# Scores in two steps for each pair of heads instead of three, with another division of the eight PSUM banks

## The chip, the cores and the metric

The kernel runs on one core of one Trainium2 chip. The metric is the device time of one execution in microseconds. The engines' names in the profile are PE (TensorE, its weight loads shown apart as PEld), DVE (VectorE), ACT (ScalarE), POOL (GpSimd) and SP (SyncE, which here only issues DMAs).

## The reference

A trunk of two layers over 512 positions of width 1024, and a last RMSNorm. In each layer one projection of the normalized input feeds three causal mixers, whose gated outputs are projected, merged by sigmoid gates, projected again and added to the input. All data is float32.

```python
def hybrid_layer(x, positions, ...):
    h = rmsnorm(x, norm_g)
    proj = jnp.einsum('bsd,dc->bsc', h, w_in)
    aq, ak, av, az, buv, bz, cq, ck, cv, cz, gl = split_cols(proj)
    ...
    oa = diff_attention(qa, ka, va, lam)      # A: 4 heads, two softmaxes each
    ya = (rmsnorm(oa, subln_g) * (1.0 - lam_init)).reshape(B, S, A_WIDTH) * jax.nn.silu(az)
    ...
    yb = u * mixed.reshape(B, S, B_WIDTH) * jax.nn.silu(bz)      # B: spatial gating
    ...
    yc = oc.reshape(B, S, C_WIDTH) * jax.nn.silu(cz)             # C: 8 heads, dilated windows
    pb = jnp.einsum('nbsc,ncd->nbsd', jnp.stack([ya, yb, yc]), w_branch)
    merged = jnp.einsum('bsnd,nbsd->bsd', jax.nn.sigmoid(gates), pb)
    return x + jnp.einsum('bsd,de->bse', merged, w_out)
```

In A, `p0 - lam * p1` of two causal softmaxes multiplies v. In C the three dilated patterns come out as one softmax with a count of 0 to 3 at each position.

## The kernel before

**Dense work.** Every float32 product is made of three matmuls of rounded parts (`mm3`, L412: high by high, high by low, low by high). The weights come from HBM in units of 512 KB (`raw`, two buffers, L151). `weights` (L176) splits each into six slots `whi`, `wlo` ahead of its use: ACT rounds (L170), DVE or POOL subtracts (L171). Most projections of two column blocks use Strassen's scheme with seven products (`seven`, L507); their weights come as one "S" group, for which `weights` takes two more buffers, `t12` and `t34`, from the tag "pr", and forms sums in them (L192 to L195). The tag "pr" has two buffers, and the softmax of the attention uses the same two. `seven` also uses one of the two buffers of the tag "sh" for as long as it runs.

**Order.** `plan` (L50) lists the items of a layer: the value projections (`i_vb`, `i_val`, all four position blocks at once in four PSUM banks), projections and attention A, attention C, then gates, branch outputs and the output projection. The attention functions call `fill`, which pulls a fixed share (`budget / FILLS`) of the dense items between their own steps, and `need`, which pulls until an item that they use is done. Tile's scheduler orders the instructions of each engine by priority before the run; scores (L870) and weight splits are lifted by 300 places.

**Attention.** `attention_a` and `attention_c` run over four pairs of heads, and over three steps for each pair, `STEPS = ((0, 1), (2,), (3,))`: the query blocks of 128 whose scores are made together. Block i has (i + 1) * 128 keys. In `scores` each block has six matmuls, three for each head of the pair (64 rows of the array each), into the two banks of one `ps_s`. DVE adds the mask and finds the row maximum (L882), ACT takes the exponential (L886); A then joins the two heads (L897) and C scales each (L904). One step later the result is transposed on PE (L910), copied by ACT (A, L935) or split by ACT and DVE (C, L418 and L419), and multiplied by v (L941, L1015). In C the two halves of the query positions are written to one bank for each head, and both banks are emptied after block 3 (L1023, L1024).

**PSUM.** Eight banks: `ps_pj` two, `ps_s` one tile of two, `ps_to` four. The sums of the first norm also pass through `ps_s` (`rms_spread`, L400): a bank of it holds the broadcast norm until ACT has copied it to `rbc` (L577).

Of the kernel before, what the change touches and what calls it, by code (L numbers as in the profile page):

```python
# [19 lines left out]
P = 128  # L20
# [16 lines left out]
FILLS = 25  # L37
STEPS = ((0, 1), (2,), (3,))
# [62 lines left out]
def hybrid_kernel(ctx: ExitStack, tc, xT, posr, wpack, tabs, cvec, pvec, rvec, lamv, sguw, outT):  # L101
# [16 lines left out]
    to_p = pool("to", bufs=4, space=PSUM)  # L118
# [10 lines left out]
    def ps_s():  # L129

        return s_p.tile([P, 2, S], F32, tag="s", name="ps_s")

    def ps_to():
        return to_p.tile([P, S], F32, tag="to", name="ps_to")

# [416 lines left out]
    def layer(l, xu, parts):  # L552
# [197 lines left out]
        def i_gl2(n, d):  # L750
# [5 lines left out]
            yield from pair(("gl2", n, d), use, ps_pj if (n, d) in ((BR_B, 0), (BR_A, 0)) else ps_to)  # L756
# [99 lines left out]
        def scores(br, h, step, r0=None):  # L856
# [3 lines left out]
            at, w0 = {}, 0  # L860
            for i in step:
                at[i] = slice(w0, w0 + (i + 1) * P)
                w0 = at[i].stop
            for i in step:
                qs = slice(i * P, (i + 1) * P)
                W = (i + 1) * P
                for t, (a, b) in enumerate(((0, 1), (1, 0), (0, 0))):
                    for m in range(2):
                        with tc.high_priority(offset=PRIO):
                            T.matmul(  # L870
                                pss[:, m, at[i]], lhsT=q[HALF[m], a, qs], rhs=k[HALF[m], b, :W], start=t == 0,
                                stop=t == 2,
                            )
            pr = t4k("pr", 2)
            rds = {}
            for i in step:
# [3 lines left out]
                for m in range(2):  # L880
                    o = pr[:, m, at[i]]
                    V.tensor_tensor_reduce(  # L882
                        out=o, in0=pss[:, m, at[i]], in1=tab[:, 0 if br == BR_A else 1, S - W :], op0=ALU.add,
# [7 lines left out]
                if br == BR_A:  # L891
# [6 lines left out]
                        out=pr[:, 0, at[i]], in0=pr[:, 1, at[i]], scalar=c, in1=pr[:, 0, at[i]], op0=ALU.mult,  # L898
                        op1=ALU.add,
                    )  # L900
                else:
                    for m in range(2):
                        o = pr[:, m, at[i]]
                        A.activation(out=o, in_=o, func=AF.Copy, scale=rd[:, m : m + 1])  # L904
            return {i: (pr[:, :, at[i]], rds[i]) for i in step}
# [7 lines left out]
        def attention_a(fill):  # L913
# [4 lines left out]
            for n in range(13):  # L918
                cur = None
                if n < 12:  # L920
                    h, step = n // 3, STEPS[n % 3]
                    need(*(("pp", BR_A, i_) for i_ in NEEDS[h]))
                    if n % 3 == 0:
                        po = ps_to().rearrange("p (i e) -> p i e", i=4)
# [4 lines left out]
                if prev is not None:  # L929
                    h, prs, po_, r0_, so_ = prev  # L930
                    pTs = {}
                    for i, (pr, rd) in prs.items():
                        pt = transposed(pr, 0, i)
                        pTs[i] = pT = att.tile([P, 4, P], F32, tag="pth", bufs=3, name="pT")
                        A.activation(out=pT[:, : i + 1, :], in_=pt, func=AF.Copy)  # L935
                    if late and 0 not in prs:
                        late.pop(0)()
                    fill()
                    for i, pT in pTs.items():
# [10 lines left out]
                    if 3 in prs:  # L950
# [21 lines left out]
                        late.extend((lambda: ons.append(scaled()), finish))  # L972
# [3 lines left out]
        def attention_c(fill):  # L976
# [3 lines left out]
            for n in range(13):  # L980
                cur = None
                if n < 12:
                    h, step = n // 3, STEPS[n % 3]
                    need(*(("pp", BR_C, i_) for i_ in NEEDS[h]))
                    if n % 3 == 0:
                        po = [ps_to() for _ in range(2)]
                    if n % 3 < 2:
                        pts = []
                        for m in range(2):
                            ph = att.tile([P, 4, 256], F32R, tag="pth", bufs=3, name="pth")  # L990
                            pl = att.tile([P, 4, 256], F32R, tag="ptl", bufs=3, name="ptl")
                            for t in (ph, pl):
                                G.memset(t[:, step[0] + 1, 0:P].bitcast(F32), 0.0)
                            pts.append((ph, pl))
                    cur = (h, scores(BR_C, h, step), po, pts)
# [3 lines left out]
                if prev is not None:  # L999
                    h, prs, po_, pts_ = prev  # L1000
                    for m in range(2):
                        for i, (pr, _) in prs.items():
                            pt = transposed(pr, m, i)
                            o = slice((i % 2) * P, (i % 2 + 1) * P)
                            split(pts_[m][0][:, : i + 1, o], pts_[m][1][:, : i + 1, o], pt)
                        fill(0.5)
                    i = max(prs)
                    if i % 2:
                        need(("val", BR_C))
                        v = val[BR_C]  # L1010
                        c = slice((i - 1) * P, (i + 1) * P)
                        for m in range(2):
                            for j in range(i + 1):
                                for s_, pt in enumerate(pts_[m]):
                                    T.matmul(  # L1015
                                        po_[m][:, c], lhsT=v[:, j, 2 * h + m, :], rhs=pt[:, j, :],
                                        start=j + s_ == 0, stop=j == i and s_ == 1,
                                    )
                    if i == 3:
                        need(("pp", BR_C, NEEDS_Z[h]))  # L1020
                        ob = t2k("ob")
                        for m in range(2):
                            A.activation(out=ob[HALF[m]], in_=po_[m][64:128], func=AF.Copy)  # L1023
                            V.tensor_tensor(out=ob[HALF[m]], in0=po_[m][0:64], in1=ob[HALF[m]], op=ALU.add)  # L1024
                        V.scalar_tensor_tensor(
                            out=yf[:, h, :], in0=ob, scalar=0.5, in1=qk[BR_C, h, "z"], op0=ALU.mult, op1=ALU.mult
                        )
# [131 lines left out]
```

## Time and profile before

| | before |
|---|---|
| median of 3 runs | 1108.19 us (1108.16 to 1108.91) |
| time of the profiled execution | 1109.62 us |
| its span, first to last instruction | 1107.9 us |
| PE busy / weight loads (PEld) busy | 1084.2 us (98%) / 938.0 us (85%) |
| DVE, ACT, POOL busy | 813.7 us (73%), 605.9 us (55%), 472.4 us (43%) |
| instructions | 17842 |

A busy engine is one with an instruction of its own running. The span of a matmul runs to its modelled end, so the spans of neighbours overlap, and how fast PE goes is read from the starts.

### The profile page before, as it was taken

How to read it: one execution, taken by the hardware profiler on the slowest of the kernel's cores; microseconds unless marked ns; L12 is line 12 of the kernel's file. 1: busy time of each engine (PE TensorE's matmuls, PEld its weight loads, DVE VectorE, ACT ScalarE, POOL GpSimd, SP SyncE). 2: the span in 40 equal slices, each digit the busy share in tenths (PEclk: the TensorE clock that was granted, in tenths of full speed). 3: DMA queues.
4: the chain of work that ended last, by engine and by line, in shares of the span. 5: the costliest groups of instructions: out<-in, count | busy, mean ns of one | idle time of the engine just before them, and what ended most of it. 6: DMA issues, size and time to landing. Idle time of an engine off the chain costs nothing.

```text
span 1107.9 us, 17842 instructions
## 1 busy us (share of the span) xinstructions
PE 1084.2 (98%) x6452; PEld 938.0 (85%) x6452; DVE 813.7 (73%) x1512; ACT 605.9 (55%) x1313; POOL 472.4 (43%) x418
## 2 busy tenths in 40 slices
PE   7999999999998999999999999999999999999997
PEld 6887878878887999998888888888788889999886
DVE  6678878877969877775427768788688797787544
ACT  6654757586774444444434456575867654444430
POOL 4004343433524766653310344534343446667420
PEclk9999999999999999999999999999999999999998
DMA  5431313220312333344523213122112133323433
GB/s 196 136 123 58 96 58 96 87 66 20 115 39 77 96 114 90 101 137 153 188 95 114 95 45 109 58 96 77 58 39 76 58 97 113 100 93 112 135 110 100
DMA packets 35064, 105.97 MB, mean 96 GB/s; under 512 B 4704, under 2 KB 7776, under 8 KB 34976
## 3 DMA queue, kind: packets, MB, share of 16 engines
q1 hardware_dynamic: 29936, 98.50, 27.9%
q10 hardware_dynamic: 5040, 6.34, 1.8%
q8 instruction: 51, 0.84, 0.3%
q14 instruction: 37, 0.30, 0.1%
HBM read 100.58 MB, written 4.24 MB: 95 GB/s over the span
## 4 chain that ended last, share of the span: by engine, by line
PE 88%; DVE 5%; issue 2%; DMA 2%; ACT 2%; POOL 1%; SPq 0%; POOLq 0%; DVEq 0%; ACTq 0%
PE ps_pj L413 15%; PE ps_pj L415 15%; PE ps_pj L414 15%; PE ps_to L415 8%; PE ps_to L413 8%; PE ps_to L414 8%; PE ps_s L870 3%; PE ps_to L910 2%; PE ps_to L440 2%; PE ps_to L438 2%; PE ps_to L439 2%; PE ps_to L1015 1%; PE ps_to L941 1%; DVE wlo L171 1%; DMA raw<-in_wpack 1%
## 5 line engine op out<-in xcount | busy, mean ns | idle before, releaser
L170 ACT ACTIVATE whi<-raw 128x512 fp32r<-128x512 f32 x316 | 194.8, 627 | 244.6 <-DMA raw<-in_wpack 81.5
L171 DVE TENSOR_TENSOR wlo<-raw,whi 128x512 fp32r<-128x512 f32 x261 | 221.5, 856 | 100.2 <-ACT whi L170 87.9
L413 PE MATMUL ps_pj<-xh,whi 128*128 128x512 f32 (+1 forms) x544 | 209.2, 385 | 0.3 <-DVE z L466 0.3
L415 PE MATMUL ps_pj<-xh,wlo 128*128 128x512 f32 (+1 forms) x544 | 204.7, 376 | 0.0
L414 PE MATMUL ps_pj<-xl,whi 128*128 128x512 f32 (+1 forms) x544 | 204.4, 376 | 0.0
L171 POOL TENSOR_TENSOR wlo<-raw,whi 128x512 fp32r<-128x512 f32 x55 | 78.5, 1428 | 156.0 <-ACT whi L170 135.9
L413 PEld LDWEIGHTS ps_pj<-xh,whi 128*128 128x128 f32 x544 | 102.6, 189 | 19.2 <-issue 1.5
L414 PEld LDWEIGHTS ps_pj<-xl,whi 128*128 128x128 f32 x544 | 102.6, 189 | 18.1 <-issue 2.4
L415 PEld LDWEIGHTS ps_pj<-xh,wlo 128*128 128x128 f32 x544 | 102.4, 188 | 18.0 <-issue 0.7
L171 DVE TENSOR_TENSOR wlo<-t,whi 128x512 fp32r<-128x512 f32 x88 | 79.8, 924 | 17.5 <-ACT whi L170 17.2
L413 PE MATMUL ps_to<-mh,whi 128*128 128x256 f32 x320 | 90.9, 284 | 0.0
L415 PE MATMUL ps_to<-mh,wlo 128*128 128x256 f32 x320 | 90.1, 284 | 0.7 <-DVE wlo L171 0.7
L886 ACT ACTIVATE pr<-pr,nm 128x128 f32<-128x128 f32 (+3 forms) x128 | 70.7, 554 | 36.9 <-DVE nm L882 36.2
L414 PE MATMUL ps_to<-ml,whi 128*128 128x256 f32 x320 | 90.5, 283 | 0.0
L170 ACT ACTIVATE whi<-t 128x512 fp32r<-128x512 f32 x112 | 65.2, 624 | 42.8 <-DVE t L193 22.9
L456 POOL TENSOR_TENSOR rsh<-rsh,sinr 128x512 f32<-128x512 f32 x32 | 42.2, 1318 | 96.9 <-DVE rsh L454 75.7
L415 PE MATMUL ps_to<-xh,wlo 128*128 128x256 f32 x240 | 67.9, 284 | 2.9 <-DVE wlo L171 1.5
L413 PE MATMUL ps_to<-xh,whi 128*128 128x256 f32 x240 | 67.8, 283 | 0.0
L414 PE MATMUL ps_to<-xl,whi 128*128 128x256 f32 x240 | 67.8, 283 | 0.0
L882 DVE CUSTOM_DVE_ANT_0 pr<-ps_s,tab 128x128 f32<-128x128 f32 (+3 forms) x128 | 56.2, 484 | 11.2 <-PE ps_s L870 7.5
L413 PEld LDWEIGHTS ps_to<-mh,whi 128*128 128x128 f32 x320 | 61.4, 192 | 0.8 <-ACT whi L170 0.2
L415 PEld LDWEIGHTS ps_to<-mh,wlo 128*128 128x128 f32 x320 | 61.1, 192 | 1.1 <-DVE wlo L171 0.9
(238 smaller groups left out, 2846.4 us busy)
## 6 DMA issues: line engine op xcount, KB each, us to landing
raw<-in_wpack SPq DMA_DIRECT2D x174, 512.0 KB
xf<-in_xT SPq DMA_DIRECT2D x8, 256.0 KB
xr<-in_xT ACTq DMA_DIRECT2D x8, 256.0 KB
x1d<-xf SPq DMA_DIRECT2D x8, 256.0 KB
raw<-in_wpack SPq DMA_DIRECT2D x4, 256.0 KB
xr<-x1d ACTq DMA_DIRECT2D x4, 256.0 KB
xr<-x1d ACTq DMA_DIRECT2D x8, 128.0 KB
out<-xf SPq DMA_DIRECT2D x8, 128.0 KB
```

The costliest lines, as they stand in the source:

```text
L170: newest[0] = A.activation(out=hi, in_=src, func=AF.Copy).ins
L171: r = (G if on_g else V).tensor_tensor(out=lo, in0=src, in1=hi.bitcast(F32), op=ALU.subtract)
L413: T.matmul(ps, lhsT=wh, rhs=mh, start=first, stop=False)
L414: T.matmul(ps, lhsT=wh, rhs=ml, start=False, stop=False)
L415: T.matmul(ps, lhsT=wl, rhs=mh, start=False, stop=last)
L438: T.matmul(banks[tb], lhsT=mh_[:, ts], rhs=wh, start=kc == 0, stop=False)
L439: T.matmul(banks[tb], lhsT=ml_[:, ts], rhs=wh, start=False, stop=False)
L440: T.matmul(banks[tb], lhsT=mh_[:, ts], rhs=wl, start=False, stop=kc == KC - 1)
L456: G.tensor_tensor(out=sh, in0=sh, in1=sinr, op=ALU.mult)
L870: T.matmul(pss[:, m, at[i]], lhsT=q[HALF[m], a, qs], rhs=k[HALF[m], b, :W], start=t == 0, stop=t == 2,)
L882: V.tensor_tensor_reduce(out=o, in0=pss[:, m, at[i]], in1=tab[:, 0 if br == BR_A else 1, S - W :], op0=ALU.add, op1=ALU.min, scale=-0.125, ...
L886: A.activation(out=o, in_=o, func=AF.Exp, scale=-1.0, bias=nm[:, m : m + 1], accum_out=den[:, m : m + 1],)
```

## The change

Scores are made in two steps for each pair of heads: blocks 0, 1 and 2 together, and block 3. `ps_s` gets a third bank, and `ps_to` is left with three. Of the large step, blocks 0 and 2 of a head share a bank (128 + 384 columns), block 1 of the first head has the middle bank, and block 1 of the second head has a bank of `ps_to`. The probabilities of block 1 go to a tile `pr1` of the tag "sh". Attention then has 8 steps and 17 shares of dense work instead of 12 and 25. In A, the scaled outputs are taken from PSUM in the step that made them. In C each half of the query positions has a bank of its own for both heads, taken when it is needed and emptied at once. The value projections take other banks, and one product of four in the gates takes a bank of `ps_s`.

```diff
-FILLS = 25
-STEPS = ((0, 1), (2,), (3,))
+FILLS = 17
+STEPS = ((0, 1, 2), (3,))
+NS = len(STEPS)
...
-    to_p = pool("to", bufs=4, space=PSUM)
+    to_p = pool("to", bufs=3, space=PSUM)
...
-        return s_p.tile([P, 2, S], F32, tag="s", name="ps_s")
+        return s_p.tile([P, 3, S], F32, tag="s", name="ps_s")
...
+    def ps_gl():
+
+        turn[0] += 1
+        return ps_to() if turn[0] % 4 else ps_s()[:, 0, :]
...
-            banks = [ps_to() for _ in range(4)]
+            banks = [ps_to() for _ in range(3)] + [ps_pj()]
             yield from proj_M(banks, xu.pair, {1: norm_sum, 4: spread})
...
-                ps2 = ps_s()
-                banks = [ps_pj(), ps_pj(), ps2[:, 0, :], ps2[:, 1, :]]
+                ps3 = ps_s()
+                banks = [ps3[:, b, :] for b in range(3)] + [ps_pj()]
...
-            banks = [ps_to() for _ in range(4)]
+            banks = [ps_to() for _ in range(3)] + [ps_pj()]
             yield from proj_M(banks, xu.pair, {kc: partial(mix, kc) for kc in range(KC)})
...
-            yield from pair(("gl2", n, d), use, ps_pj if (n, d) in ((BR_B, 0), (BR_A, 0)) else ps_to)
+            yield from pair(("gl2", n, d), use, ps_pj if (n, d) in ((BR_B, 0), (BR_A, 0)) else ps_gl)
...
             pss = ps_s()
-            at, w0 = {}, 0
+            pr = t4k("pr", 2)
+            if step == (3,):
+                at = {(m, 3): pss[:, 2 * m, :] for m in range(2)}
+                to = {3: pr}
+            else:
+                pr1 = t2k("sh", name="pr1").rearrange("p (m k) -> p m k", m=2)
+                at = {(m, 0): pss[:, 2 * m, 0:P] for m in range(2)}
+                at |= {(0, 1): pss[:, 1, :256], (1, 1): ps_to()[:, :256]}
+                at |= {(m, 2): pss[:, 2 * m, P:S] for m in range(2)}
+                to = {0: pr[:, :, 0:P], 1: pr1, 2: pr[:, :, P:S]}
...
-                        pTs[i] = pT = att.tile([P, 4, P], F32, tag="pth", bufs=3, name="pT")
+                        pTs[i] = pT = att.tile([P, 4, P], F32, tag=("ptl", "pth", "pth", "ptl")[i], bufs=3, name="pT")
...
-                    if late and 0 not in prs:
+                    if late:
                         late.pop(0)()
                     fill()
+                    if 0 in prs:
+                        po_.append(ps_to().rearrange("p (i e) -> p i e", i=4))
+                    po_ = po_[0]
...
-                        late.extend((lambda: ons.append(scaled()), finish))
+                        ons.append(scaled())
+                        late.append(finish)
```

In `attention_c`, after the change, from where a finished step is taken up (lines that are as before are cut):

```python
                    for i, (pr, _) in prs.items():
                        if i % 2 == 0:
                            pts = []
                            for m in range(2):
                                ...
                                for t in (ph, pl):
                                    G.memset(t[:, i + 1, 0:P].bitcast(F32), 0.0)
                                pts.append((ph, pl))
                        for m in range(2):
                            pt = transposed(pr, m, i)
                            ...
                        fill(0.5)
                        if i % 2 == 0:
                            continue
                        ...
                        po = ps_to().rearrange("p (m c) -> p m c", m=2)
                        ...
                        c = slice((i - 1) * P, (i + 1) * P)
                        if i == 1:
                            ob = t2k("ob")
                        for m in range(2):
                            A.activation(out=ob[HALF[m], c], in_=po[64:128, m, :], func=AF.Copy)
                            V.tensor_tensor(out=ob[HALF[m], c], in0=po[0:64, m, :], in1=ob[HALF[m], c], op=ALU.add)
```

## Rows read from the trace of the kernel before

**Rows 1.** The page: busy time of each engine, and the last chain by engine.

```profile
PE 1084.2 (98%) x6452; PEld 938.0 (85%) x6452; DVE 813.7 (73%) x1512; ACT 605.9 (55%) x1313; POOL 472.4 (43%) x418
...
PE 88%; DVE 5%; issue 2%; DMA 2%; ACT 2%; POOL 1%; SPq 0%; POOLq 0%; DVEq 0%; ACTq 0%
```

**Rows 2.** Windows: stretch, its length, busy time of each engine, clock, DMA.

```profile
25.00:96.00 71.00, 70.93 (x312) 57.80 (x312) 52.00 (x88) 36.60 (x63) 9.52 (x7) 1.00 0.38 125
...
96.00:350.00 254.00, 249.36 (x1524) 209.79 (x1523) 202.17 (x446) 166.91 (x414) 105.55 (x112) 1.00 0.23 71
350.00:545.00 195.00, 195.00 (x1232) 177.36 (x1231) 139.40 (x200) 89.63 (x164) 112.99 (x79) 1.00 0.38 121
638.00:895.00 257.00, 251.63 (x1542) 212.49 (x1541) 205.28 (x446) 168.00 (x416) 107.95 (x113) 1.00 0.22 70
```

**Rows 3.** Timeline of PE and PEld around one group of scores: start, length, instruction.

```profile
103.54 0.39 PE L415 MATMUL ps_pj<-xh,wlo 128*128 128x512 f32 x1
103.77 0.39 PE L413 MATMUL ps_pj<-xh,whi 128*128 128x512 f32 x1
104.09 0.79 PE L870 MATMUL ps_s<-k,q 64*128 64x384 f32 x6
104.80 0.50 PE L414 MATMUL ps_pj<-xl,whi 128*128 128x512 f32 x1
105.14 0.39 PE L415 MATMUL ps_pj<-xh,wlo 128*128 128x512 f32 x1
...
105.14 0.19 PEld L413 LDWEIGHTS ps_pj<-xh,whi 128*128 128x128 f32 x1
```

**Rows 4.** The last chain in order of time: start, length, groups of block 2 and block 3.

```profile
181.05 0.72 PE ps_s L870 x6
185.93 0.89 PE ps_s L870 x6
```

**Rows 5.** Timeline, layer 0: from the first value projection to the copied norm.

```profile
31.13 0.39 PE L438 MATMUL ps_pj<-whi,xuh 128*128 128x512 f32 x1
...
32.04 1.02 PE L409 MATMUL ps_s<-dg,ones 128*128 128x512 f32 x2
...
32.88 1.89 ACT L170 ACTIVATE whi<-raw 128x512 fp32r<-128x512 f32 x3 [4.03 <-DMA raw<-in_wpack]
...
34.68 1.84 ACT L585 ACTIVATE vb<-ps_to,rp 128x512 f32<-128x512 f32 x3
...
37.48 0.62 ACT L577 ACTIVATE rbc<-ps_s 128x512 f32<-128x512 f32 x1
...
38.15 0.50 PE L438 MATMUL ps_s<-whi,xuh 128*128 128x512 f32 x1
```

**Rows 6.** The same place in layer 1.

```profile
567.77 0.60 ACT L577 ACTIVATE rbc<-ps_s 128x512 f32<-128x512 f32 x1 [1.32 <-PE ps_s L409]
...
574.85 0.39 PE L438 MATMUL ps_pj<-whi,xuh 128*128 128x512 f32 x1
```

**Rows 7.** Timeline of POOL: the first and the last of eight such pairs in attention.

```profile
113.19 1.29 POOL L192 TENSOR_TENSOR t<-raw 128x512 f32<-128x512 f32 x1 [2.85 <-PE ps_to L910]
...
117.90 1.29 POOL L194 TENSOR_TENSOR t<-raw 128x512 f32<-128x512 f32 x1
...
865.71 1.30 POOL L192 TENSOR_TENSOR t<-raw 128x512 f32<-128x512 f32 x1 [0.22 <-PE ps_to L910]
...
869.27 1.30 POOL L194 TENSOR_TENSOR t<-raw 128x512 f32<-128x512 f32 x1 [2.27 <-PE ps_to L910]
```

**Rows 8.** What PE waited for, in all: total us, times, longest.

```profile
PE ps_to L1015 <- DVE ptl L419: 1.2, 2, 0.7
...
PE ps_to L1015 <- DVE ob L1024: 0.2, 1, 0.2
```

**Rows 9.** Groups by line and shape: busy us, mean ns, idle time before.

```profile
L1024 DVE TENSOR_TENSOR ob<-ps_to,ob 64x512 f32<-64x512 f32 x16 | 10.9, 681 | 6.2 <-ACT ob L1023 6.1
L532 DVE TENSOR_TENSOR eb<-ps_to,ea 128x256 f32<-128x256 f32 x40 | 16.5, 416 | 4.0 <-PE ps_to L415 3.6
```

More of the change, by code (lines that the diff above doesn't have):

```diff
@@ L870, in scores @@
                             T.matmul(
-                                pss[:, m, at[i]], lhsT=q[HALF[m], a, qs], rhs=k[HALF[m], b, :W], start=t == 0,
-                                stop=t == 2,
+                                at[m, i], lhsT=q[HALF[m], a, i * P : (i + 1) * P], rhs=k[HALF[m], b, : (i + 1) * P],
+                                start=t == 0, stop=t == 2,
                             )
-            pr = t4k("pr", 2)
             rds = {}
@@ L897, in scores @@
                     V.scalar_tensor_tensor(
-                        out=pr[:, 0, at[i]], in0=pr[:, 1, at[i]], scalar=c, in1=pr[:, 0, at[i]], op0=ALU.mult,
+                        out=to[i][:, 0, :], in0=to[i][:, 1, :], scalar=c, in1=to[i][:, 0, :], op0=ALU.mult,
                         op1=ALU.add,
@@ L902, in scores @@
                     for m in range(2):
-                        o = pr[:, m, at[i]]
+                        o = to[i][:, m, :]
                         A.activation(out=o, in_=o, func=AF.Copy, scale=rd[:, m : m + 1])
-            return {i: (pr[:, :, at[i]], rds[i]) for i in step}
+            return {i: (to[i], rds[i]) for i in step}
         def transposed(pr, m, i):
@@ L917, in attention_a @@
             prev = None
-            for n in range(13):
+            for n in range(4 * NS + 1):
                 cur = None
-                if n < 12:
-                    h, step = n // 3, STEPS[n % 3]
+                if n < 4 * NS:
+                    h, step = n // NS, STEPS[n % NS]
                     need(*(("pp", BR_A, i_) for i_ in NEEDS[h]))
-                    if n % 3 == 0:
-                        po = ps_to().rearrange("p (i e) -> p i e", i=4)
+                    if n % NS == 0:
+                        po = []
                         r0 = sm.tile([P, 4, 2], F32, tag="r0", bufs=2, name="r0")
@@ L979, in attention_c @@
             prev = None
-            for n in range(13):
+            for n in range(4 * NS + 1):
                 cur = None
-                if n < 12:
-                    h, step = n // 3, STEPS[n % 3]
+                if n < 4 * NS:
+                    h, step = n // NS, STEPS[n % NS]
                     need(*(("pp", BR_C, i_) for i_ in NEEDS[h]))
[L985 to L995, printed above, removed]
+                    cur = (h, scores(BR_C, h, step))
                     fill()
@@ L999, in attention_c @@
                 if prev is not None:
-                    h, prs, po_, pts_ = prev
-                    for m in range(2):
-                        for i, (pr, _) in prs.items():
+                    h, prs = prev
+                    for i, (pr, _) in prs.items():
+                        if i % 2 == 0:
+                            pts = []
+                            for m in range(2):
+                                ph = att.tile([P, 4, 256], F32R, tag="pth", bufs=3, name="pth")
+                                pl = att.tile([P, 4, 256], F32R, tag="ptl", bufs=3, name="ptl")
+                                for t in (ph, pl):
+                                    G.memset(t[:, i + 1, 0:P].bitcast(F32), 0.0)
+                                pts.append((ph, pl))
+                        for m in range(2):
@@ L1017, in attention_c @@
                                         start=j + s_ == 0, stop=j == i and s_ == 1,
                                     )
-                    if i == 3:
-                        need(("pp", BR_C, NEEDS_Z[h]))
-                        ob = t2k("ob")
+                        c = slice((i - 1) * P, (i + 1) * P)
+                        if i == 1:
+                            ob = t2k("ob")
                         for m in range(2):
[L1023 to L1027, printed above, removed]
+                            A.activation(out=ob[HALF[m], c], in_=po[64:128, m, :], func=AF.Copy)
+                            V.tensor_tensor(out=ob[HALF[m], c], in0=po[0:64, m, :], in1=ob[HALF[m], c], op=ALU.add)
@@ L1028, in attention_c @@
+                        if i == 3:
+                            need(("pp", BR_C, NEEDS_Z[h]))
+                            V.scalar_tensor_tensor(
+                                out=yf[:, h, :], in0=ob, scalar=0.5, in1=qk[BR_C, h, "z"], op0=ALU.mult, op1=ALU.mult
+                            )
                 prev = cur
```

20 lines of the change are left out of this document (7 added, 13 removed).

## The prediction

> **What bounds the kernel now.** I read the page first. PE has something running in 98% of the span, and the chain that ended last lies on PE for 88% of it [rows 1]. The windows then show where PE is idle: not at all in the 195 us of gates and branch outputs of layer 0, but 254 - 249.36 = 4.6 us and 257 - 251.63 = 5.4 us in the two stretches of attention, 10.0 us together [rows 2]. The clock stands at 1.00 in all of them. Last I read PE's timeline, since spans overlap and only starts tell its pace. Dense matmuls of 512 columns start 0.23 us apart, and around a group of scores this pace breaks [rows 3]. So the kernel is bound by PE's stream, and the change can act in three ways: by the breaks around scores, by the 10 us of idle, and by new waits.
>
> One rule of the Trainium skill would read this otherwise. "Perfetto Trace Analysis", section Identifying the Most-Contended Engine, judges TensorE by weight loads and not by matmul spans; the 85% here [rows 1] would then leave 15% of slack, the breaks would be worth nothing, and the sum below would be 2.0 us slower than before. The trace disagrees: undisturbed matmuls of 512 columns have one load of 0.19 us in each 0.23 us [rows 3], 83%, and nothing is being waited for.
>
> **The breaks, taken out 16 times.** Block 2 had a group of its own, four pairs of heads in two branches of two layers: 16 groups. One of them is priced by PE's timeline [rows 3]. From the dense matmul at 103.77 to the second dense start after it, 105.14, there are 1.37 us; the two dense ones in this need 2 x 0.23, so the scores cost 0.92. How much of that is flow? The groups of 384 and of 512 columns take 0.72 and 0.89 us [rows 4]: 0.17 us for three pairs of 128 columns more, 0.057 for each (an estimate). Three pairs of 384 columns are then 3 x 3 x 0.057 = 0.51 us of flow, and 0.92 - 0.51 = 0.41 us are break: the start 0.09 late, the first pair, the end, the first dense matmul behind. In a common group the start, the end and the dense one behind go. A first-pair wait can stay, because block 2 brings other query weights: inside the group, 0.72 - 0.51 = 0.21 us are not flow, the end and the first pair in one. I let half of that stay: 0.41 - 0.11 = 0.30 us saved, with 0.20 and 0.41 as bounds. 16 x 0.30 = **4.8 us less** (3.2 to 6.6).
>
> The Trainium skill, "TensorEngine Tiling (Array Packing)", section Key Properties, says that PE drains when the tiling mode changes, and names no such cost for a new block in the same mode. By that the first-pair wait would go too and the saving be the upper bound; the traced groups [rows 3, 4] show breaks only where the mode changes and can't tell the two apart.
>
> **The start of layer 0.** The value projection of A took two banks of `ps_pj` and the two of `ps_s`; now it takes three of `ps_s` and one of `ps_pj`. `ps_s` is closed there until ACT has copied the broadcast norm out of it. PE makes the broadcast at 32.04, but ACT first rounds three weight pieces that waited for a DMA until 32.88, and empties the banks of the projection before; the copy runs at 37.48, and the first matmul into `ps_s` at 38.15 [rows 5]. Meanwhile, from 31.13, PE did 27 matmuls into `ps_pj`. These are nine threes, over two position blocks and so over five weight pieces. With one open bank in place of two PE can do only one block's, five threes or 15. The other 12 are late: 12 x 0.227 = **2.7 us more**. Nothing behind it before attention makes it good, since PE has only 0.07 us of idle from 25 to 96 us [rows 2]. The lower bound is nothing: ACT's order may put the copy ahead of the emptying. I take 2.7, since the copy becomes ready after the work now ahead of it, which the change leaves as it is. In layer 1 the copy ends at 568.4, over 6 us before the first value matmul of A at 574.85 [rows 6]: nothing. The two other value projections exchange one bank of `ps_to` for one of `ps_pj` that was emptied an item earlier: nothing.
>
> **Branch C's output.** Both heads had a bank each for the whole pair; now one bank is held from its first matmul to its emptying. PE's recorded waits in L1015 are 1.2 + 0.2 = 1.4 us [rows 8]. Each share of dense work that lies between a split and the matmuls that need it grows from 1/25 to 1/17 of the same budget, which covers more of them: I take half, **0.7 us less** (0 to 1.4). The halves cost more instructions: for each pair of heads four additions of 0.416 us (128 x 256 from PSUM being the nearest row) in place of two of 0.681 [rows 9], 0.30 us more; for four pairs in two layers 2.4 us on DVE, and I put the same on ACT. They cost nothing where they lie under dense matmuls: DVE is idle 52 us in each stretch of attention [rows 2]. Without that cover they are 2.4 us.
>
> **What I cost at nothing.** Fewer and larger shares of dense work: same sum. DVE's first read waits for 18 matmuls instead of 12, some 0.6 us, under the share that follows. Block 1 of the second head needs a free `ps_to`; PE holds all that is queued behind it, so a late bank is a stall or a group in two parts, priced below. In A the four scaled copies on ACT now follow POOL's three small operations at once; behind them wait weight roundings, which run six slots ahead of PE. POOL's memsets of C's split tiles are issued when the first block of a half is taken up; POOL's own queue, with its weight subtractions, waits behind them for the multiplication before. No step that moves issues a DMA; SP's loads wait for `raw` as before. In the gates three banks of `ps_to` and one of `ps_s` still make four. The output projection has three banks, each filled by 24 matmuls (5.4 us): nothing.
>
> **Sum.** -4.8 + 2.7 - 0.7 = -2.8 us on a profiled execution of 1109.62 (span 1107.9 and 1.7 around it). That execution was 1.4 us above the median; on the median of 1108.19 the same difference gives **1105.4**. Its own range: 6.6 and 1.4 saved and no loss at the start, 1100.2; 3.2 saved, 2.7 and 2.4 lost, 1110.1.
>
> **Rivals.** *The weights wait longer (slower).* S groups share the two buffers of "pr" with the softmax. L192 writes the first of them and L194 the second; undisturbed, L194 follows after L192's own 1.3 us. In attention it follows after 4.7 us in the first pair and 3.6 in the last [rows 7]; over the eight pairs (four in each layer) it is 45.7 us, of which 45.7 - 8 x 1.3 = 35.3 are waiting for the next release, by transposes on PE. SP can't reload `raw` meanwhile. With 8 steps for 12 the releases lie 1.5 times as far apart: 17.6 us more waiting. Six slots ahead cover most of it; today's idle of 10.0 us is 0.28 of the waiting, so 5.0 us at the least if that share holds, 17.6 if none of the addition is covered. That is 1110.4 to 1123.0; I take **1112**, near the share that the rows show. It decides from 5.0 us of new idle on (2.8 gained and 2.2 of measurement), 0.6 for each pair. Against it: the releaser is PE's own transposition, which can go as soon as its softmax is done.
>
> *The groups fall apart (no change).* If the bank of `ps_to` for the second head's block 1 comes late, or the scheduler places block 2 by itself, the 18 matmuls run in two groups in half of the cases: -2.4 + 2.7 - 0.7, **1107.8**.
>
> *The waiting shrinks (much faster).* Each branch now asks for "pr" eight times, not twelve, and C has a third bank for transpositions where its two output banks left two. If a third of the idle goes, 3.3 us, and the copy at the start comes early: -4.8 - 0.7 - 3.3, **1099.4**.
>
> **How the numbers follow.** A measurement of this kernel tells about 0.2%, 2.2 us, from no change: faster is below 1106.0, slower above 1110.4. The sum has 0.42 (faster 0.28, same 0.13, slower 0.01), the weights' wait 0.27 (slower 0.25, same 0.02), the falling apart 0.18 (same 0.13, faster 0.02, slower 0.03), the shrinking 0.13 (faster). Faster 0.43, same 0.28, slower 0.29. The range runs from 1099, at the much faster rival, to 1114, in the upper part of the slower one.
>
> **What would show it.** Right: in the trace after, 32 groups of L870, half of them of 18 matmuls in a row, with one late start each; PE waiting at about 33 to 38 us for `rbc`; idle of PE in attention near 10 us. Wrong: L192 to L194 further apart in attention than 45.7 us in all, and PE idle behind them on `wlo`; groups of 12 and 6; no wait at 33 to 38 us, or one longer than 2.7 us; PE idle in the gates, where three banks and one would then not be four.

## The result, and the profile after

| | time | against before, 95% interval |
|---|---|---|
| before, measured beside it | 1108.55 us | |
| the changed kernel | 1162.98 us (1160.32 to 1164.0, 4 runs) | 1.0481 [1.0468, 1.0494] |

The change makes the kernel 4.8% slower, 54 us. The kernel before took 1108.55 to 1109.93 us beside the runs of this document, on several chips, so differences between runs carry up to 1.4 us of that. The prediction of 1105.4 us and its range up to 1114 are both missed, and so are the prices of all rivals.

The page of the changed kernel answers to [rows 1]:

```profile
PE 1104.8 (95%) x6452; PEld 954.7 (82%) x6452; DVE 820.6 (71%) x1528; ACT 608.7 (52%) x1329; POOL 472.9 (41%) x418
...
PEclk9999998989998999999999999999898999999999
...
PE 81%; ACT 7%; DVE 6%; issue 3%; POOL 2%; DMA 1%; POOLq 0%; DVEq 0%; SPq 0%; ACTq 0%
```

PE has the same 6452 matmuls. ACT's share of the last chain goes from 2% to 7%, and the granted clock is no longer full in all slices. To see where, I cut both kernels at the first score, at the last product with v in A and at the last one in C. The windows of the kernel before, so cut (A and C of layer 0, A and C of layer 1; columns as in [rows 2]):

```profile
97.30:210.00 112.70, 112.17 (x681) 94.24 (x681) 92.11 (x209) 70.03 (x189) 48.20 (x44) 1.00 0.24 75
210.00:329.10 119.10, 118.56 (x716) 99.08 (x715) 88.53 (x205) 85.25 (x205) 48.96 (x64) 1.00 0.19 61
639.80:752.90 113.10, 112.79 (x683) 94.88 (x683) 91.85 (x210) 70.51 (x190) 48.58 (x44) 1.00 0.22 72
752.90:873.60 120.70, 118.21 (x713) 99.06 (x712) 92.10 (x205) 84.59 (x205) 48.98 (x63) 1.00 0.19 61
```

The same four stretches of the changed kernel, and the one from the gates of layer 0 to the first score of layer 1:

```profile
99.20:226.80 127.60, 120.50 (x706) 101.65 (x706) 97.59 (x215) 71.57 (x192) 48.95 (x44) 0.97 0.22 72
226.80:355.40 128.60, 118.60 (x688) 99.02 (x687) 88.11 (x209) 84.54 (x209) 46.28 (x62) 0.95 0.15 47
667.50:794.70 127.20, 119.11 (x707) 99.77 (x706) 95.41 (x215) 71.93 (x192) 48.13 (x45) 1.00 0.22 71
794.70:927.30 132.60, 121.40 (x698) 102.11 (x697) 89.79 (x209) 84.94 (x209) 46.49 (x63) 0.92 0.14 45
...
374.40:667.50 293.10, 293.10 (x1672) 258.01 (x1670) 196.42 (x285) 133.35 (x235) 130.80 (x93) 1.00 0.36 116
```

The four stretches take 516.0 us in place of 465.6, 50.4 us more for 2799 matmuls against 2793. PE's busy time in them is 479.6 us against 461.7; its idle time is 36.4 us against 3.9. So 32.5 us are new idle time and 17.9 us are matmuls that run longer. (The 10.0 us of idle that the prediction read in wider windows lie for 6.1 us behind the last product of C.) Outside attention little moved: the spans differ by 1161.4 - 1107.9 = 53.5 us, and the gates still have no idle.

Why matmuls run longer is seen in the windows of changed clock (columns as above, the clock is the third from the end):

```profile
180.00:186.40 6.40, 3.84 (x31) 3.41 (x30) 1.85 (x2) 2.89 (x7) 4.33 (x5) 1.00 0.31 83
186.40:193.20 6.80, 5.42 (x24) 4.39 (x24) 6.69 (x26) 5.79 (x20) 1.12 (x2) 0.50 0.27 85
251.30:261.50 10.20, 7.79 (x26) 6.52 (x27) 6.29 (x15) 5.49 (x14) 3.38 (x6) 0.50 0.17 53
...
821.30:831.50 10.20, 8.29 (x27) 6.96 (x28) 6.13 (x14) 4.99 (x13) 3.37 (x6) 0.50 0.18 53
```

In six stretches, 47.6 us in all, the granted clock is 0.50, the 1.2 GHz level (the last microseconds, where it is 0.50 in both kernels, left out); each begins after PE has stood with gaps (before 186.4 it was busy for 3.84 of 6.40 us, before the other five for 2.42 to 4.65 of as many). Five of them lie in the four stretches of attention, with 33.0 us of busy time. At half the pace half of that, 16.5 us, is extra PE time; by the starts of one product at both levels (0.12 and 0.21 us apart, shown at the end) it is some 14. Both are estimates, near the 17.9. The Trainium skill, "TensorE: Matmul & The Clock Gate", Part 1, says that the clock is gated by how busy PE has been; the trace agrees so far, 0.50 only behind such gaps. But not each of them brings the clock down: at the same place in layer 1, from 748.9 to 755.3, PE was busy for 3.84 of 6.40 us too, and the clock stayed at 1.00.

**Where the idle comes from.** The timeline of the changed kernel, all engines, around two of the eight S groups in attention; L200 and L202 are the former L192 and L194 [rows 7], L178 and L179 the rounding and the subtraction of the weights, L421 a dense matmul, L882 the scores, L893 the softmax's first step, L908 its last in A, L921 the transposition, L946 the copy of the transposed block:

```profile
169.06 1.27 POOL L200 TENSOR_TENSOR t<-raw 128x512 f32<-128x512 f32 x1 [0.60 <-PE ps_to L921]
...
169.36 1.52 DVE L908 SCALAR_TENSOR_TENSOR pr<-pr,c 128x512 f32<-128x512 f32 x1
...
178.84 0.92 PE L882 MATMUL ps_s<-k,q 64*128 64x256 f32 x10
...
181.22 0.60 PE L921 MATMUL ps_to<-ident,pr 128*128 128x128 f32 x4
...
181.85 0.60 ACT L946 ACTIVATE pT<-ps_to 128x512 f32<-128x512 f32 x1 [3.01 <-PE ps_to L921]
...
181.90 1.27 POOL L202 TENSOR_TENSOR t<-raw 128x512 f32<-128x512 f32 x1 [5.08 <-PE ps_to L921]
...
183.20 1.15 ACT L178 ACTIVATE whi<-t 128x512 fp32r<-128x512 f32 x2 [0.75 <-POOL t L202]
...
184.38 1.79 DVE L179 TENSOR_TENSOR wlo<-t,whi 128x512 fp32r<-128x512 f32 x1 [5.57 <-ACT whi L178]
...
185.12 0.37 ACT L543 ACTIVATE ea<-ps_pj 128x256 f32<-128x256 f32 x1
...
185.54 0.39 PE L421 MATMUL ps_pj<-mh,whi 128*128 128x256 f32 x1 [1.88 <-ACT ea L543]
...
186.34 0.29 DVE L893 CUSTOM_DVE_ANT_0 pr<-ps_s,tab 128x128 f32<-128x128 f32 x1 [0.17 <-POOL so L965]
...
189.15 1.22 PE L882 MATMUL ps_s<-k,q 64*128 64x512 f32 x4 [1.38 <-DVE nm L893]
...
864.39 1.30 POOL L200 TENSOR_TENSOR t<-raw 128x512 f32<-128x512 f32 x1
...
878.45 1.27 POOL L202 TENSOR_TENSOR t<-raw 128x512 f32<-128x512 f32 x1 [0.46 <-PE ps_to L921]
```

Follow the first of them. `t12` gets its buffer of "pr" at 169.06. `t34` must wait for the next transposition, and gets its own 12.8 us later, at 181.90. That transposition's softmax was done at 170.88 (169.36 + 1.52). PE comes to the transposition only at 181.22, 10.3 us later, because a share of dense work and the 18 scores of the next step stand before it in PE's order. From there the wait goes on to the other engines. DVE stands for 5.57 us before the subtraction of weights; ACT stands for 3.01 us before the copy of that transposed block and 0.75 us before the rounding. Behind these in the same queues wait ACT's emptying of a `ps_pj` bank, without which PE stands for 1.88 us, and DVE's next softmax: the 18 scores were made by 179.8, and their softmax begins at 186.34. So the weights wait for PE to release the softmax's buffer, and then PE and the next softmax wait behind the weights. That this in turn lengthens a later wait for "pr" the trace does not show. Over the eight groups, L200 to L202 are 75.4 us apart (8.35, 12.84, 12.55, 3.43, 6.65, 12.84, 14.06, 4.64), against 45.7 before. The releasing transpositions start 4.1 to 10.6 us after their softmax is done, 62 us in all; before it was 1.3 to 6.5, 36 in all. In C another queue has a part: of the 14.1 us between the last two rows POOL stands 10.8 us before `memset`s of C's split tiles, which come ahead of L202.

What waits for what in the changed kernel, in all (total us, times, longest), beside [rows 8]:

```profile
POOL t L202 <- PE ps_to L921: 18.3, 6, 5.1
...
PE ps_to L921 <- DVE ptl L427: 9.8, 4, 4.3
```

The second row is another loss, at the start of C. PE's, ACT's and DVE's timeline there:

```profile
248.25 0.60 PE L921 MATMUL ps_to<-ident,pr 128*128 128x128 f32 x4
252.81 0.69 PE L921 MATMUL ps_to<-ident,pr 128*128 128x128 f32 x2 [3.97 <-DVE ptl L427]
...
251.21 0.62 ACT L178 ACTIVATE whi<-raw 128x512 fp32r<-128x512 f32 x1
251.73 0.69 ACT L426 ACTIVATE pth<-ps_to 128x128 fp32r<-128x128 f32 x3
...
252.47 0.81 DVE L427 TENSOR_TENSOR ptl<-ps_to,pth 128x128 fp32r<-128x128 f32 x3
```

PE has filled the three banks of `ps_to` with transposed blocks and stands before the next one, while ACT does scales, exponentials and roundings first and begins to empty the banks at 251.73.

### The profile page after: what moved, and what is told of

The parts are those of the page before. It is cut to its first block, busy times and chain, and to the rows that moved or that the text cites. A ratio compares the mean times of both kernels' runs of the same rounds, so it can differ in the third digit from the quotient of the medians.

```text
span 1161.4 us, 17877 instructions
## 1 busy us (share of the span) xinstructions
PE 1104.8 (95%) x6452; PEld 954.7 (82%) x6452; DVE 820.6 (71%) x1528; ACT 608.7 (52%) x1329; POOL 472.9 (41%) x418
## 4 chain that ended last, share of the span: by engine, by line
PE 81%; ACT 7%; DVE 6%; issue 3%; POOL 2%; DMA 1%; POOLq 0%; DVEq 0%; SPq 0%; ACTq 0%
PE ps_pj L421 13%; PE ps_pj L422 13%; PE ps_pj L423 13%; PE ps_to L423 7%; PE ps_to L421 7%; PE ps_to L422 7%; ACT pr L897 2%; PE ps_s L882 2%; PE ps_to L446 2%; PE ps_to L447 2%; PE ps_to L448 2%; PE ps_to L921 2%; PE ps_s L421 1%; ACT whi L178 1%; PE ps_s L423 1%
## 5 line engine op out<-in xcount | busy, mean ns | idle before, releaser
L178 ACT ACTIVATE whi<-raw 128x512 fp32r<-128x512 f32 x316 | 195.5, 628 | 275.1 <-PE ps_pj L422 76.7
L179 DVE TENSOR_TENSOR wlo<-raw,whi 128x512 fp32r<-128x512 f32 x261 | 220.9, 853 | 127.4 <-ACT whi L178 111.6
L421 PE MATMUL ps_pj<-xh,whi 128*128 128x512 f32 (+1 forms) x544 | 208.2, 383 | 4.3 <-DVE t L463 1.8
L179 POOL TENSOR_TENSOR wlo<-raw,whi 128x512 fp32r<-128x512 f32 x55 | 77.9, 1416 | 168.2 <-ACT whi L178 155.1
L421 PEld LDWEIGHTS ps_pj<-xh,whi 128*128 128x128 f32 x544 | 103.7, 191 | 25.6 <-DVE t L463 2.6
L422 PEld LDWEIGHTS ps_pj<-xl,whi 128*128 128x128 f32 x544 | 103.7, 191 | 17.6 <-issue 1.1
L179 DVE TENSOR_TENSOR wlo<-t,whi 128x512 fp32r<-128x512 f32 x88 | 83.4, 963 | 35.5 <-ACT whi L178 35.4
L178 ACT ACTIVATE whi<-t 128x512 fp32r<-128x512 f32 x112 | 66.0, 624 | 44.7 <-DVE t L201 24.0
L897 ACT ACTIVATE pr<-pr,nm 128x128 f32<-128x128 f32 (+3 forms) x128 | 70.5, 553 | 24.2 <-DVE nm L893 24.2
L423 PE MATMUL ps_to<-mh,wlo 128*128 128x256 f32 x240 | 67.8, 283 | 0.4 <-DVE wlo L179 0.4
L421 PE MATMUL ps_to<-mh,whi 128*128 128x256 f32 x240 | 68.2, 284 | 0.0
L422 PE MATMUL ps_to<-ml,whi 128*128 128x256 f32 x240 | 67.8, 283 | 0.0
L893 DVE CUSTOM_DVE_ANT_0 pr<-ps_s,tab 128x128 f32<-128x128 f32 (+3 forms) x112 | 50.8, 495 | 15.3 <-PE ps_s L882 14.9
L795 POOL TENSOR_TENSOR acc<-acc,zs 128x512 f32<-128x512 f32 x32 | 50.8, 1599 | 18.9 <-DVE zs L794 17.7
L540 POOL TENSOR_TENSOR zs<-zs,eb 128x256 f32<-128x256 f32 x28 | 29.5, 1054 | 66.4 <-DVE eb L540 46.2
L421 PE MATMUL ps_pj<-mh,whi 128*128 128x256 f32 x128 | 41.8, 327 | 12.4 <-ACT ea L543 6.9
L202 POOL TENSOR_TENSOR t<-raw 128x512 f32<-128x512 f32 x28 | 43.4, 1549 | 23.7 <-PE ps_to L921 18.3
L421 PE MATMUL ps_to<-xh,whi 128*128 128x256 f32 x180 | 51.2, 285 | 1.9 <-ACT whi L178 1.9
```

Source lines behind the costliest of these rows:

```text
L178: newest[0] = A.activation(out=hi, in_=src, func=AF.Copy).ins
L179: r = (G if on_g else V).tensor_tensor(out=lo, in0=src, in1=hi.bitcast(F32), op=ALU.subtract)
L202: SE[2].tensor_tensor(out=s3, in0=a11, in1=a21, op=ALU.subtract)
L421: T.matmul(ps, lhsT=wh, rhs=mh, start=first, stop=False)
L422: T.matmul(ps, lhsT=wh, rhs=ml, start=False, stop=False)
L423: T.matmul(ps, lhsT=wl, rhs=mh, start=False, stop=last)
```

## The experiments

Two theories stand against each other. *The weights wait*: fewer and longer steps hold the two "pr" buffers longer, S groups wait for them, and what stands behind the waiting weights makes the idle. *Order and banks*: the order of the two steps and the new division of PSUM cost by themselves, whoever uses "pr". A third, in one run, was that C's `memset`s stand in POOL's queue ahead of weights. All ratios are against the kernel before, measured on the same chip.

**The steps alone.** The changed code with three steps, in all other respects the changed kernel:

```diff
-FILLS = 17
-STEPS = ((0, 1, 2), (3,))
+FILLS = {"A": 25, "C": 25}
+THREE = ((0, 1), (2,), (3,))
+STEPS_A = THREE
+STEPS_C = THREE
```

> The changed kernel with the old three steps (blocks 0 and 1, block 2, block 3; 25 shares), in the new banks: three for scores, three of ps_to, C's output emptied in halves. If the two steps are what costs (the waits for 'pr', or the order of the transpositions), this goes back to 1106 to 1113 us, with idle of PE in attention near 10 us. If the new division of the banks costs by itself, it stays above 1140 us.

Measured: 1132.9 us, 1.0209 [1.019, 1.0229], between the two forecasts. This was a badly set control. The new C calls `fill` less often, so of 25 shares only 20 were pulled in it. With C in 21 shares (`"C": 21`):

> The changed kernel in three steps again, with the budget of C's dense work in 21 shares: in the run before, C pulled only 20 of its 25 shares, since a step of one block now pulls half a share where it pulled two halves. If that thin cover made C slow there (C with the gating took 147 us in layer 0, 136 in the kernel before), this goes to 1108 to 1116 us. If C's own new code or the banks do, it stays at 1125 to 1135.

Measured: 1119.26 us, 1.0085 [1.007, 1.01], 3 us above the first forecast and 6 below the second. The thin cover was most of what made C slow there, and something is left. Two steps therefore cost 1163.0 - 1119.3 = 43.7 us, and what is left of the change 9.

**The banks alone.** As the last one, but with the old division: two score banks, four of `ps_to`, the old banks in value projections and gates.

```diff
-    to_p = pool("to", bufs=3, space=PSUM)
+    to_p = pool("to", bufs=4, space=PSUM)
...
-        return s_p.tile([P, 3, S], F32, tag="s", name="ps_s")
+        return s_p.tile([P, 2, S], F32, tag="s", name="ps_s")
```

> The same three steps and 21 shares with the old division of the banks everywhere (two of scores, four of ps_to, the value projections and gates as before). What is left of the change is C's output in halves, its split tiles taken later, and A's outputs scaled at once. If the third bank of ps_to's loss costs, this is 10 us or more faster than with the new banks; if C's new code costs, it is within 4 us of it and over 1120.

Measured: 1109.91 us, 1.0002 [0.9993, 1.0012]. C's output in halves, its split tiles taken late and A's early scaling together cost nothing that can be measured; the division of the banks costs 9.35 us. The windows of the two kernels tell only in part where. Branch C of both layers with three banks of `ps_to`,

```profile
213.50:336.20 122.70, 119.51 (x716) 99.10 (x715) 90.43 (x214) 86.82 (x211) 46.66 (x62) 1.00 0.17 52
...
760.80:884.90 124.10, 119.87 (x716) 99.11 (x715) 92.08 (x213) 87.95 (x212) 48.66 (x63) 1.00 0.18 56
```

and with four:

```profile
211.40:331.30 119.90, 117.28 (x703) 97.43 (x702) 92.48 (x215) 85.99 (x211) 47.18 (x62) 1.00 0.19 58
...
754.80:873.90 119.10, 116.15 (x691) 96.02 (x691) 91.36 (x213) 87.41 (x212) 47.82 (x63) 1.00 0.20 61
```

The first score of layer 0 comes 2.1 us later (98.9 against 96.8). C is 2.8 and 5.0 us longer, but its windows also hold 13 and 25 matmuls more, which the later stages then no longer have to do. PE's idle in C grows only from 2.6 + 3.0 to 3.2 + 4.2 us. So the 7.8 us are not all a loss of C, and where the rest of the 9.35 arises stays open.

**No S groups in attention.** The changed kernel, with the four Strassen groups of each layer that meet attention as plain products (eight where Strassen's scheme has seven). The same values are computed, with more matmul work and without `t12` and `t34`:

```diff
+EIGHT |= {("u2", 0), ("u2", 2), ("pp", BR_C, 5), ("gl2", BR_A, 0)}
```

> The changed kernel with the four Strassen groups of each layer that meet attention (u2 0, u2 2, the last of C's projections, the first gate of A) done as plain projections; same results. No group then takes the buffers of 'pr' during attention. The plain form costs PE about 0.9 us more for each of the eight groups, 7 us in all. Theory 'the weights wait for pr': idle of PE in attention falls from 41 us to 10 to 15, the clock stays up, 1115 to 1130 us. Theory 'order and banks': the stalls behind transpositions stay, above 1145 us.

Measured: 1127.31 us, 1.0165 [1.0145, 1.0186]: 35.7 us of the loss gone, although PE has more to do. PE's idle in the four stretches falls from 36.4 to 14.9 us, and none of that is left in A. The clock does not stay up all the time as *the weights wait* expected: it is 0.95 in C of layer 0 and 0.99 in C of layer 1. What is left is named first by its waits:

```profile
PE ps_to L922 <- DVE ptl L428: 8.3, 2, 4.3
```

the stall at the start of C, once in each layer. The fourth corner, the same line added to the three steps with 21 shares:

> Three steps in the new banks with branch C in 21 shares (1119.3 us so far), and the four Strassen groups that meet the attention as plain matmuls. It is the fourth corner beside the changed kernel (1163.0), the changed kernel without those groups (1127.3) and three steps with them (1119.3). Theory 1, the weights wait for the shared staging tiles and two steps make that wait long: without such weights the number of steps hardly matters, and three steps gain only what they waited themselves: 1108 to 1116 us, so that two steps cost 44 us with the groups and 11 to 19 without. Theory 2, the order of two steps costs by itself, through full banks of transpositions, whoever uses the staging tiles: the same 44 us between two and three steps without the groups, so about 1083 us.

Measured: 1119.02 us, 1.0079 [1.0065, 1.0093].

| | S groups in attention | plain products there |
|---|---|---|
| two steps | 1162.98 | 1127.31 |
| three steps, same banks | 1119.26 | 1119.02 |

The second step saved costs 43.7 us where S groups share "pr", and 8.3 us where none does. The order of the steps alone would have cost the same in both columns. Plain products do without `seven`, and so also free its buffer of the tag "sh", which `pr1` uses too; the next runs change "pr" alone. Both forecasts for the last corner missed, *the weights wait* by 3 us (it expected three steps to gain some 3 to 11 us too), *order and banks* by 36. That three steps gain nothing here is not explained by a run; its trace has PE busy for 1096.0 us against 1089.8 with S groups, and a clock of 0.97 in C of layer 1 against 1.00.

**A third "pr" buffer.** It does not fit in SBUF beside six weight slots, so a control with five slots goes with it:

```diff
-NSLOT = 6
+NSLOT = 5
...
-                    t12, t34 = t4k("pr", 2, name="t12"), t4k("pr", 2, name="t34")
+                    t12, t34 = t4k("pr", 3, name="t12"), t4k("pr", 3, name="t34")
...
-            pr = t4k("pr", 2)
+            pr = t4k("pr", 3)
```

> The changed kernel with five weight slots instead of six, only as the control of the run with three buffers of 'pr', which needs the room. Both theories: the same as the changed kernel or somewhat slower, 1163 to 1180 us; 'the weights wait for pr' expects the upper part, since one piece less covers the wait.

> The changed kernel with three buffers of 'pr' and five weight slots. Theory 'the weights wait for pr': L200 to L202 closer together in attention (75 us in all for the eight pairs now, below 50 then), and at least 20 us faster than the control with five slots. Theory 'order and banks': within 8 us of that control.

Measured: the control (first hunk alone) 1171.88 us, 1.0567 [1.0538, 1.0596]; with the third buffer 1139.92 us, 1.0279 [1.0258, 1.03]. Nothing but the buffer differs, and 32 us are gone. The windows of A and C of layer 0 and A and C of layer 1, in the control and then with the buffer:

```profile
100.60:236.40 135.80, 125.99 (x707) 106.19 (x707) 95.66 (x214) 72.37 (x192) 48.49 (x44) 0.92 0.21 67
236.40:365.60 129.20, 118.59 (x688) 98.73 (x687) 89.95 (x210) 84.90 (x209) 45.94 (x62) 0.95 0.16 50
678.90:805.40 126.50, 119.69 (x707) 100.51 (x706) 96.12 (x214) 71.83 (x192) 48.83 (x44) 0.99 0.23 71
805.40:938.80 133.40, 122.42 (x701) 102.46 (x700) 89.82 (x211) 86.35 (x211) 49.83 (x63) 0.92 0.16 52
```

```profile
100.30:219.20 118.90, 117.03 (x706) 99.54 (x706) 96.47 (x214) 71.50 (x192) 51.37 (x44) 1.00 0.24 76
219.20:349.20 130.00, 120.17 (x723) 101.62 (x722) 91.66 (x216) 87.17 (x213) 48.51 (x64) 0.96 0.19 58
655.20:776.40 121.20, 118.61 (x706) 100.51 (x706) 94.86 (x214) 71.98 (x192) 49.88 (x44) 0.99 0.23 74
776.40:906.80 130.40, 121.20 (x723) 101.80 (x722) 91.72 (x215) 86.59 (x212) 49.75 (x64) 0.96 0.19 57
```

PE's idle in A falls from 9.8 + 6.8 = 16.6 us to 1.9 + 2.6 = 4.5. In C it falls only from 10.6 + 11.0 = 21.6 to 9.8 + 9.2 = 19.0, although C then holds some more matmuls. One forecast of *the weights wait* was missed: L200 to L202 of the eight groups are still 59.6 us apart, not under 50. Two of them, 17.6 and 18.1 us, lie in C, where L202 no longer waits for "pr" but stands behind `memset`s in POOL's queue. So the shared buffer is shown as the cause in A; in C it is a smaller part.

**Which branch.** Two steps in one branch and three in the other, with 17 shares for two steps, and 25 (A) or 21 (C) for three:

```diff
+STEPS_A = TWO
+STEPS_C = THREE
```

> Two steps in branch A (17 shares), three in branch C (21 shares), new banks, all Strassen groups as in the changed kernel. Between three_c21 (1119.3) and the changed kernel (1163.0) lie 43.7 us. Theory 1 (weights wait): six of the eight groups' weights in the attention fall in A or at the turn from A to C, so A carries over half: 1141 to 1150. Theory 2 (banks filled by transpositions at the start of C): A has no such stall, and two steps cost in A a third at most: 1119 to 1134.

```diff
+STEPS_A = THREE
+STEPS_C = TWO
```

> Three steps in branch A (25 shares), two in branch C (17 shares), new banks, all Strassen groups as in the changed kernel. Theory 1 (weights wait): C carries less than half of the 43.7 us: 1132 to 1141, and the pairs of group sums that lie far apart are those in C alone. Theory 2 (banks filled by transpositions at the start of C): C carries most of it: 1148 to 1163.

Measured: two steps in A 1143.46 us, 1.0305 [1.0292, 1.0319]; in C 1136.55 us, 1.0245 [1.023, 1.0261]. Against 1119.26 that is 24.2 and 17.3 us, together 41.5 of the 43.7: both as *the weights wait* expected. With two steps in C alone, the pairs of sums that lie far apart are the two of C (12.5 and 14.4 us, in A 3.8 to 9.2), as that theory said too. A has no stall on the split tiles and carries the larger part. C's 17.3 us hold also the stall at its start, 8.3 us in the run without S groups.

**POOL's queue.** Three steps with 21 shares, and C's `memset`s on DVE, because POOL's wait for a free split tile (44.7 us before, 87.2 after) stands ahead of its weight work:

```diff
-                                    G.memset(t[:, i + 1, 0:P].bitcast(F32), 0.0)
+                                    V.memset(t[:, i + 1, 0:P].bitcast(F32), 0.0)
```

> Three steps, 21 shares, new banks, and the zeros of C's split tiles written by DVE instead of POOL. In the changed kernel POOL stands 47 us in C's stretch of layer 0 before these writes, waiting for PE's multiplication (24 before), with the rotations of the next projections queued behind. If that queue is what slows C, this is at least 8 us faster than the run with 21 shares; otherwise within 4 us.

Measured: 1130.7 us, 1.0187 [1.0167, 1.0208], 11.4 us slower than with POOL, which neither forecast had. For three steps the wait is worse at the head of DVE's queue than of POOL's. The run changes both queues at once, though, and was not made with two steps, where POOL's wait is the long one; for C with two steps that theory stays open.

**The kernel before without its own waits.** If S groups wait for "pr" even with three steps [rows 7], plain products should help the kernel before, which has the old banks. First the two late groups, then all four:

```diff
+EIGHT |= {("pp", BR_C, 5), ("gl2", BR_A, 0)}
```

> The kernel before, with the last projection of C and the first gate of A as plain projections; same results. The four groups at the end of C in two layers stood beside 7 to 10 of the 10 us of PE's idle in attention; the plain form costs 4 x 0.9 us. 'The weights wait for pr': 3 to 7 us faster than before, 1101 to 1105. 'Order and banks': 2 to 5 us slower.

```diff
+EIGHT |= {("u2", 0), ("u2", 2), ("pp", BR_C, 5), ("gl2", BR_A, 0)}
```

> The kernel before with all four Strassen groups that meet the attention as plain matmuls, and nothing else changed (with the two late ones alone plain it took 1102.6). Theory 1 (weights wait): the four weights that wait at the start of A go too; by their waits in the trace of before (35 us in all, most of it hidden) against some 14 us of TensorE work that the plain groups add: 1098 to 1106. Theory 2 (banks, not staging): plain groups only add work on TensorE, so 1108 to 1118.

Measured: 1102.55 us, 0.9941 [0.9919, 0.9963], and 1102.45 us, 0.9936 [0.9924, 0.9948]. Both beat the kernel before by 0.6%, little but outside the interval, as *the weights wait* expected, and the changed one by 5%. The other two groups, at the start of A, neither gain nor lose. Why the new banks swallow this gain was not tried.

## Why the prediction was wrong

**The step that failed.** The sum put the new waits for "pr" at nothing, and the rival *The weights wait longer*, which named the mechanism, had its size wrong. Four steps in it fell.
- The release. The argument held against the rival, that the releasing transposition "can go as soon as its softmax is done", is false. In the group followed above PE came to it 10.3 us after that, and in all eight groups 4.1 to 10.6 us. Even in the kernel before it was 1.3 to 6.5 us. What delays the release is PE's own order: the next scores and the share of dense work, which the change made 25/17 as large.
- The waiting. L192 to L194 in all were to come to 45.7 + 17.6 = 63.3 us, by steps 1.5 times as long. They came to 75.4, so the waiting is 75.4 - 8 x 1.3 = 65.0 us, 1.84 times the 35.3. Part of that is that the steps themselves became longer than by their work: 516.0 / 32 = 16.1 us against 465.6 / 48 = 9.7, 1.66 times.
- The share of it that PE feels. I took 0.28 of the waiting and priced the rival near its lower bound of 5.0 us. New idle is 32.5 us for 29.7 us of new waiting, but not all of it belongs to the weights: 14.9 us of idle stay when no S group meets attention, and the kernel before had 3.9. So an estimate of the weights' part is 36.4 - 14.9 - 3.9 = 17.6 us, 0.59 of the new waiting. That it equals the upper bound of the rival is chance. I had asked only when the weights are late for PE, with six slots ahead as cover. I had not asked what stands behind the waiting rounding and subtraction on ACT and DVE: the emptying of banks and the softmax itself. For A's scaled copies I even wrote that weight roundings wait behind them, and did not turn the question round.
- The clock was taken as 1.00 throughout, as it was before. It stands at the 1.2 GHz level for 47.6 us, which makes PE's matmuls in attention some 14 to 16.5 us longer (an estimate) and stood in no case. How much of this is lost time is not shown: A of layer 0, with 6.8 us at 0.50, took 127.6 us, and A of layer 1, with none, 127.2.

**Costed at nothing, and not nothing:** the banks, 9.35 us with three steps. About 2.1 of it is the start of layer 0, which the sum had; the rest it did not have. The sentence on the shrinking waits, that C has a third bank where two output banks left two, compared the wrong things: with the outputs in halves four banks would have been there, and the runs show four against three. I priced a late bank only as groups in two parts; with two steps it shows as PE standing before a transposition (3.97 and 4.35 us at the start of C).

**What held.** The groups of scores did not fall apart: 32 of them, 18 and 6 matmuls in turn. What the 16 breaks saved cannot be read beside the loss. At the start of layer 0 the timeline of the changed kernel shows, in answer to [rows 5],

```profile
30.11 0.39 PE L446 MATMUL ps_pj<-whi,xuh 128*128 128x512 f32 x1
...
33.00 0.51 PE L446 MATMUL ps_pj<-whi,xuh 128*128 128x512 f32 x1 [0.50 <-ACT whi L178]
...
36.50 0.50 PE L446 MATMUL ps_pj<-whi,xuh 128*128 128x512 f32 x1 [0.89 <-ACT whi L178]
...
36.91 0.61 ACT L585 ACTIVATE rbc<-ps_s 128x512 f32<-128x512 f32 x1
...
37.57 0.49 PE L446 MATMUL ps_s<-whi,xuh 128*128 128x512 f32 x1
```

From 30.11 there are 18 matmuls in `ps_pj`, six threes where five were forecast, and then `ps_s` from 37.57. With 27 before, 9 are late and not 12, about 2.0 us; the first score comes at 99.2 in place of 97.3 us, 1.9 late where 2.7 were forecast. The recorded waits there are for `whi`, not for `rbc`. The gates have no idle with three banks and one. The halves of C's output cost nothing, as the run with the old banks shows.

**The accounts.** Of 54.4 us, 9 are the banks (three steps with the old and the new division). Some 43.7 are the two steps. Of these, 35 go when no S group meets attention (43.7 - 8.3). The 8.3 left are as much as PE's two waits for the split tiles in that kernel; that they are the same was not tried. How the waits and the clock share the 35, and how much of C's part is POOL's queue, was not tried either.

## What to carry to other kernels

Before making a step longer, list who else takes the buffers that the step holds, and for each of them what stands behind its waiting instruction in every engine's queue. Ask also when the releasing instruction comes in the order of its own engine, and not only when its input is ready: here that was up to 10.6 us later. A buffer shared between a prefetch and the work that it runs ahead of is the first place to look: here plain products, which do without it, gained 0.6% even in the tuned kernel.

## What the runs showed of the hardware

The granted clock of PE fell to 0.50 in the middle of a stage that stands at 1.00 in the kernel before, with gaps on PE ahead of it (before 186.4 one of 1.88 us and a thin stretch; around 251.3 one of 3.97 us). The dense matmuls of 256 columns of one product then start about 0.21 us apart in place of 0.12:

```profile
186.12 0.28 PE L422 MATMUL ps_pj<-ml,whi 128*128 128x256 f32 x1
186.24 0.28 PE L423 MATMUL ps_pj<-mh,wlo 128*128 128x256 f32 x1
...
186.94 0.41 PE L421 MATMUL ps_pj<-mh,whi 128*128 128x256 f32 x1
187.15 0.41 PE L422 MATMUL ps_pj<-ml,whi 128*128 128x256 f32 x1
```

So new idle of PE can be followed by slower matmuls: here 17.9 us of longer busy time stand beside 32.5 us of idle. The two do not simply add up. In layer 1 the same gap left the clock at 1.00, and A there is only 0.4 us shorter than in layer 0.
